# Dividing PSUM in a hybrid mixer trunk: four banks for the dense products, two for the RWKV recurrence, two for the other mixers, in place of three, three and two

## The chip, the cores and the metric

The kernel runs on one core of one Trainium2 chip. The metric is the device time of one execution in microseconds (us). A core has five engines that each work through their own list of instructions: TensorE (PE; its weight loads are PEld), VectorE (DVE), ScalarE (ACT), GpSimd (POOL) and SyncE (SP), which here issues most of the transfers. TensorE writes its results to PSUM, which the kernel uses as eight banks of 128 partitions by 512 floats.

## What is computed

One layer of a trunk with four sequence mixers side by side, for one sequence of 512 tokens and width 1024, all in float32. Cut to what matters:

```python
u = rms_norm(x, g)
fa, fb, fc, fd, gates = split(u @ w_in)         # one wide projection
ya = rwkv7_mix(fa, ...)     # per head: s = s*w + sa (kk*a)^T + v k^T, y = s r
yb = gla_mix(fb, ...)       # gated linear attention in chunks
yc = mlstm_mix(fc, ...)     # matrix LSTM
yd = ssd_mix(fd, ...)       # state space mixer in chunks of 128
h  = x + sum(sigmoid(gate_i) * (y_i @ w_branch_i)) @ w_out
out = rms_norm(h + ffn(rms_norm(h)))            # ffn: 1024 -> 2 x 2816, conv of 3, silu, back
```

## The kernel before, in words

The activations lie with features on the partitions and all 512 tokens along the free axis, so a dense product is one bank: 128 output features by 512 tokens. Each float32 operand is split into a high and a low part in the fast matmul format (hi on ACT at L222, lo on VectorE or POOL at L223), and each product is three matmuls: high by high, high by low and low by high (mm3, L231 to L234). A product `fm` (L305) with 1024 input features is 24 such matmuls of 128x512 into one psd bank; `tm` (L314) makes a product with tokens on the partitions, in 128x256 pieces, with two psd banks at a time (L327 to L329); `branch` (L391) multiplies a mixer's output back to the width (psd<-ohg and olg for GLA, ohr and olr for RWKV, ohm and olm for mLSTM). All dense products take their bank from `pd()`, which is the pool psd.

The mixers stand between the dense products:

- RWKV (`rwkv_half`, L484 to L736) is done in two halves of four heads. Its matmuls take banks from `pr_()`, the pool psr: pair products (L565, L556 to L573, three banks for one pair), the inverse of a triangular matrix by 31 steps on VectorE (L597, L599), its combination (L626, L631), and then the recurrence over eight chunks (L647 to L707). In a step, psx collects the value part (zv, L650) and the carried state (L661), L663 copies it, L687 multiplies it, L690 copies the result to uu, and psy (L673, L678) collects the output, which ACT copies to Yt at L707. The next step's psx is taken right behind the copy at L690, while psy is still open. Behind the last step comes the group norm (L712 to L720), the transposes L725, the gate product L733 and L734, L735.
- GLA (`gla`) takes banks from `pm()`, the pool psm: its chunk products L821 (32x64 pieces) and L835 (64x32 pieces), then L847, L851.
- SSD (`ssd`) and mLSTM (`mlstm`) also use `pm()`, but while `wide` is set, most of their calls go to psr instead (L199 to L203). SSD makes four chunks of 128 tokens; each brings in a decay tile by transfer (sab, L1011, two buffers), works on it (L1033 on POOL and VectorE, exponent on ACT L1034, mask L1035 on POOL, L1044 on VectorE) and multiplies it (L1048), with L1023 as transposes, L1040 and L1041 as the products of the state's keys, L1054 and L1060 as the state's. `ssd_z` (the gate z of SSD, written after the SSD code) is a `tm` product that is emptied at L1077. mLSTM scans its gates (L927 to L932), sends them through DRAM (md, L935, L939), transposes them (L943, L944), makes the weights (L954 to L959), multiplies (L958, L967) and transposes its output (L978).

Everything is written in one function, `tile_trunk_kernel`, in the order RWKV half 0, GLA, SSD, branch 1, z, RWKV half 1, branch 3, mLSTM, branches 0 and 2, output projection, FFN. The order in which an engine gets its instructions is set by a scheduler of the framework, from the priorities that the code gives (`tc.high_priority` with the numbers in Q, L36), from the dependencies, and from which buffers of the pools are free. At about 868 us the three PSUM pools are closed, and the FFN takes all eight banks as one pool (psf).

Of the kernel before, what the change touches and what calls it, by code (L numbers as in the profile page):

```python
# [13 lines left out]
PSUM = bass.MemoryType.PSUM  # L14
# [146 lines left out]
def kernel(ctx: ExitStack, tc: tile.TileContext, A, out):  # L161
# [21 lines left out]
    rpad.tile([P, 56], F32, name="rpad")  # L183
    wp = ctx.enter_context(tc.tile_pool(name="wp", bufs=1))
    ps_ctx = ExitStack()
    psd = ps_ctx.enter_context(tc.tile_pool(name="psd", bufs=3, space=PSUM))
    psr = ps_ctx.enter_context(tc.tile_pool(name="psr", bufs=3, space=PSUM))
    psm = ps_ctx.enter_context(tc.tile_pool(name="psm", bufs=2, space=PSUM))
    dense = [psd]
    dr = ctx.enter_context(tc.tile_pool(name="dr", bufs=1, space=DRAM))  # L190
# [1136 lines left out]
```

## Time and profile before

| what | value |
| --- | --- |
| median of 3 runs | 1225.39 us |
| lowest, highest | 1217.79, 1230.0 us |
| profiled execution | 1220.7 us |
| its span, first to last instruction | 1218.9 us |
| mean granted TensorE clock | 0.981 |
| PE busy | 1166.5 us (96%) |
| DVE busy | 653.7 us (54%) |
| ACT busy | 445.5 us (37%) |
| POOL busy | 333.1 us (27%) |

Busy times count compute instructions alone. A matmul's own duration overlaps its neighbours' on PE, so the time from one to the next is read from a count in a window, not from the mean of one. A window of the trace gives the busy time of each engine between two times; the granted clock is a share of full speed, where 1 is the higher of the two levels (2.4 GHz) and half of it is the lower (1.2 GHz).

### The profile page before, as it was taken

How to read it: one execution, taken by the hardware profiler on the slowest of the kernel's cores; microseconds unless marked ns; L12 is line 12 of the kernel's file. 1: busy time of each engine (PE TensorE's matmuls, PEld its weight loads, DVE VectorE, ACT ScalarE, POOL GpSimd, SP SyncE). 2: the span in 40 equal slices, each digit the busy share in tenths (PEclk: the TensorE clock that was granted, in tenths of full speed). 3: DMA queues.
4: the chain of work that ended last, by engine and by line, in shares of the span. 5: the costliest groups of instructions: out<-in, count | busy, mean ns of one | idle time of the engine just before them, and what ended most of it. 6: DMA issues, size and time to landing. Idle time of an engine off the chain costs nothing.

```text
span 1218.9 us, 17897 instructions
## 1 busy us (share of the span) xinstructions
PE 1166.5 (96%) x6881; PEld 935.6 (77%) x6881; DVE 653.7 (54%) x1090; ACT 445.5 (37%) x820; POOL 333.1 (27%) x287
## 2 busy tenths in 40 slices
PE   5999989999999998989999999999999999999997
PEld 4886865777779965767877877778888888888886
DVE  5257792444675437397224654464556656562323
ACT  4355232223322533223123434342444444442323
POOL 3113110023473246241112363440122222220100
PEclk9998987999999999999999999999999999999999
DMA  5122330122332221323123532463222322323232
GB/s 203 62 88 65 83 85 25 36 83 83 97 104 70 95 90 65 81 78 109 60 72 105 190 112 87 164 217 87 79 95 95 103 96 96 95 95 100 92 102 104
DMA packets 79886, 117.30 MB, mean 96 GB/s; under 512 B 22660, under 2 KB 27172, under 8 KB 79800
## 3 DMA queue, kind: packets, MB, share of 16 engines
q1 hardware_dynamic: 79224, 115.11, 29.7%
q8 instruction: 54, 0.88, 0.3%
q10 hardware_dynamic: 576, 1.05, 0.2%
q14 instruction: 32, 0.26, 0.1%
HBM read 107.93 MB, written 8.19 MB: 95 GB/s over the span
## 4 chain that ended last, share of the span: by engine, by line
PE 74%; DVE 10%; DMA 7%; issue 4%; POOL 2%; ACT 2%; SPq 0%; POOLq 0%; DVEq 0%; ACTq 0%
PE psd L232 16%; PE psd L233 16%; PE psd L234 15%; PE psd L1276 3%; PE psd L1274 3%; PE psd L1275 3%; DVE Mt L597 2%; DVE Mi L599 2%; PE psd L328 2%; PE psd L327 2%; PE psd L329 2%; DVE lo L223 2%; DMA sab<-ad 2%; PE psr L673 1%; DMA raw<-in_wo_dram 1%
## 5 line engine op out<-in xcount | busy, mean ns | idle before, releaser
L223 DVE TENSOR_TENSOR lo<-raw,hi 128x512 fp32r<-128x512 f32 x280 | 226.7, 811 | 299.9 <-ACT hi L222 285.0
L222 ACT CAST hi<-raw 128x512 fp32r<-128x512 f32 x322 | 199.4, 620 | 495.6 <-PE psd L233 300.7
L232 PE MATMUL psd<-uh,hi 128*128 128x512 f32 (+1 forms) x912 | 364.0, 400 | 15.0 <-ACT hi L222 5.1
L234 PE MATMUL psd<-uh,lo 128*128 128x512 f32 (+1 forms) x912 | 362.7, 398 | 5.4 <-DVE lo L223 4.2
L233 PE MATMUL psd<-ul,hi 128*128 128x512 f32 (+1 forms) x912 | 360.5, 396 | 0.2 <-DVE ul L249 0.2
L232 PEld LDWEIGHTS psd<-uh,hi 128*128 128x128 f32 x912 | 173.3, 190 | 57.0 <-ACT hi L222 7.3
L234 PEld LDWEIGHTS psd<-uh,lo 128*128 128x128 f32 x912 | 173.4, 190 | 48.8 <-DVE lo L223 6.2
L233 PEld LDWEIGHTS psd<-ul,hi 128*128 128x128 f32 x912 | 173.4, 190 | 37.3 <-issue 3.1
L223 POOL TENSOR_TENSOR lo<-raw,hi 128x512 fp32r<-128x512 f32 x42 | 57.1, 1360 | 245.8 <-ACT hi L222 176.0
L1263 POOL TENSOR_TENSOR y<-y 128x512 f32<-128x512 f32 x22 | 28.3, 1288 | 172.3 <-DVE y L1257 158.4
L1257 DVE SCALAR_TENSOR_TENSOR y<-psd,pf,y 128x510 f32<-128x510 f32 x88 | 65.8, 749 | 3.0 <-issue 0.3
L1276 PE MATMUL psd<-hi,al 128*128 128x512 f32 x164 | 63.8, 389 | 0.0
L1275 PE MATMUL psd<-lo,ah 128*128 128x512 f32 x164 | 63.8, 389 | 0.0
L1274 PE MATMUL psd<-hi,ah 128*128 128x512 f32 x164 | 57.3, 389 | 0.0
L328 PE MATMUL psd<-lo,uh 128*128 128x256 f32 x192 | 56.1, 292 | 1.0 <-DVE lo L223 1.0
L327 PE MATMUL psd<-hi,uh 128*128 128x256 f32 x192 | 55.5, 289 | 0.0
L329 PE MATMUL psd<-hi,ul 128*128 128x256 f32 x192 | 55.4, 289 | 0.0
L328 PEld LDWEIGHTS psd<-lo,uh 128*128 128x128 f32 x192 | 37.0, 193 | 5.0 <-issue 3.2
L327 PEld LDWEIGHTS psd<-hi,uh 128*128 128x128 f32 x192 | 36.9, 192 | 1.9 <-issue 1.3
L329 PEld LDWEIGHTS psd<-hi,ul 128*128 128x128 f32 x192 | 37.0, 193 | 1.3 <-issue 1.0
L1275 PEld LDWEIGHTS psd<-lo,ah 128*128 128x128 f32 x164 | 30.8, 188 | 6.4
L1276 PEld LDWEIGHTS psd<-hi,al 128*128 128x128 f32 x164 | 30.8, 188 | 6.4
(418 smaller groups left out, 1725.6 us busy)
## 6 DMA issues: line engine op xcount, KB each, us to landing
raw<-in_wfm_dram SPq DMA_DIRECT2D x140, 256.0 KB, 2.6
raw<-in_up_dram SPq DMA_DIRECT2D x88, 256.0 KB, 2.5
raw<-in_dn_dram SPq DMA_DIRECT2D x44, 256.0 KB, 2.5
raw<-in_bp_dram SPq DMA_DIRECT2D x32, 256.0 KB, 2.6
raw<-in_wtm_dram SPq DMA_DIRECT2D x24, 256.0 KB, 2.6
raw<-in_wo_dram SPq DMA_DIRECT2D x16, 256.0 KB, 2.7
gd<-th SPq DMA_DIRECT2D x15, 256.0 KB, 2.1
th<-gd SPq DMA_DIRECT2D x15, 256.0 KB, 3.0
```

Source lines behind the costliest of these rows:

```text
L222: S.copy(hi, raw)
L223: eng.tensor_tensor(lo, raw, hi.bitcast(F32), op=ALU.subtract)
L232: PE.matmul(ps, lh, rh, start=first, stop=False)
L233: PE.matmul(ps, lh, rl, start=False, stop=False)
L234: PE.matmul(ps, ll, rh, start=False, stop=last)
L327: PE.matmul(o, uh[:, k, bs], hi[:, cs], start=first, stop=False)
L328: PE.matmul(o, uh[:, k, bs], lo[:, cs], start=False, stop=False)
L329: PE.matmul(o, ul[:, k, bs], hi[:, cs], start=False, stop=last)
L1257: V.scalar_tensor_tensor(y[:, d:T], ps[:, 0:T - d], col("fcw", k * 44 + n), y[:, d:T], op0=ALU.mult, op1=ALU.add)
L1274: PE.matmul(ps, ah[:, k, bs], hi, start=(k == 0), stop=False)
L1275: PE.matmul(ps, ah[:, k, bs], lo, start=False, stop=False)
L1276: PE.matmul(ps, al[:, k, bs], hi, start=False, stop=(k == NF - 1))
```

## The change

One bank goes from the pool psr to the pool psd; psm keeps its two. The sum stays at eight.

```diff
@@ -183,8 +183,8 @@
     ps_ctx = ExitStack()
-    psd = ps_ctx.enter_context(tc.tile_pool(name="psd", bufs=3, space=PSUM))
-    psr = ps_ctx.enter_context(tc.tile_pool(name="psr", bufs=3, space=PSUM))
+    psd = ps_ctx.enter_context(tc.tile_pool(name="psd", bufs=4, space=PSUM))
+    psr = ps_ctx.enter_context(tc.tile_pool(name="psr", bufs=2, space=PSUM))
     psm = ps_ctx.enter_context(tc.tile_pool(name="psm", bufs=2, space=PSUM))
```

No instruction is added or removed on PE, DVE, ACT or POOL; the scheduler puts them in another order on every engine. Three places of PE's list follow, before and after the change; psd<-uh marks a dense product, psm and psr the mixers' small ones.

GLA's chunk products L835 on PE, in the kernel before:

```order
L835 MATMUL psm<-w 32x32
L233 MATMUL psd<-ul,hi 128x512
L835 MATMUL psm<-w 32x32
L234 MATMUL psd<-uh,lo 128x512
L835 MATMUL psm<-w 32x32
L232 MATMUL psd<-uh,hi 128x512
L835 MATMUL psm<-w 32x32
L233 MATMUL psd<-ul,hi 128x512
L835 MATMUL psm<-w 32x32
```

And the same 32 products of GLA on PE in the changed kernel, with dense rows around them:

```order
L234 MATMUL psd<-uh,lo 128x512
L232 MATMUL psd<-uh,hi 128x512
L233 MATMUL psd<-ul,hi 128x512
L234 MATMUL psd<-uh,lo 128x512
L835 MATMUL psm<-w 32x32 x32
L232 MATMUL psd<-uh,hi 128x512
L233 MATMUL psd<-ul,hi 128x512
```

In the kernel before the single L835 stand one by one between dense matmuls; in the changed kernel this group of 32 is one row.

SSD on PE in the kernel before, from the second chunk's L1048 on:

```order
L234 MATMUL psd<-ohg,lo 128x512
L1048 MATMUL psm<-w,sab 128x64 x8
L1054 MATMUL psm<-w 128x256 x2
L1060 MATMUL psr<-w,sbt 128x256 x2
L1023 MATMUL psr<-cst,w 128x128 x4
L1040 MATMUL psr<-w 128x128 x2
L232 MATMUL psd<-uh,hi 128x512
L233 MATMUL psd<-ul,hi 128x512
L234 MATMUL psd<-uh,lo 128x512
L232 MATMUL psd<-uh,hi 128x512
L233 MATMUL psd<-ul,hi 128x512
L234 MATMUL psd<-uh,lo 128x512
```

SSD on PE in the changed kernel, from the last matmuls of the z product (L327 to L329) on:

```order
L327 MATMUL psd<-hi,uh 128x256
L328 MATMUL psd<-lo,uh 128x256
L329 MATMUL psd<-hi,ul 128x256
L1048 MATMUL psm<-w,sab 128x64 x4
L1060 MATMUL psm<-w,sbt 128x256 x2
L1048 MATMUL psm<-w,sab 128x64 x4
L1040 MATMUL psr<-w 128x128 x2
L1041 MATMUL psr<-cst,w 128x128 x2
L1048 MATMUL psm<-w,sab 128x64 x4
L1054 MATMUL psm<-w 128x256 x2
L1048 MATMUL psm<-w,sab 128x64 x4
L1060 MATMUL psr<-w,sbt 128x256 x2
```

The dense rows (psd<-uh, psd<-ohg) that stood between SSD's matmuls are gone from between them; the z products stand ahead. The next dense row is behind the last L1054:

```order
L1048 MATMUL psm<-w,sab 128x64 x4
L1060 MATMUL psr<-w,sbt 128x256 x2
L1041 MATMUL psm<-cst,w 128x128 x2
L1023 MATMUL psr<-cst,w 128x128 x4
L1048 MATMUL psr<-w,sab 128x64 x8
L1054 MATMUL psr<-w 128x256 x2
L232 MATMUL psd<-uh,hi 128x512
L233 MATMUL psd<-ul,hi 128x512
L234 MATMUL psd<-uh,lo 128x512
```

The L232 at its end is the start of the next RWKV half's projection.

The end of the second RWKV half on PE in the kernel before, from the last dense rows ahead of L725 on:

```order
L232 MATMUL psd<-uh,hi 128x512
L233 MATMUL psd<-ul,hi 128x512
L234 MATMUL psd<-uh,lo 128x512
L725 MATMUL psr<-cst,Yt 128x128 x8
L733 MATMUL psr<-sg,gup 128x512
L232 MATMUL psd<-uh,hi 128x512
L233 MATMUL psd<-ul,hi 128x512
L234 MATMUL psd<-uh,lo 128x512
L232 MATMUL psd<-uh,hi 128x512
L233 MATMUL psd<-ul,hi 128x512
```

The same place in the changed kernel, from the last step of the recurrence on:

```order
L687 MATMUL psr<-xs,MT 64x64 x4
L673 MATMUL psr<-uu,zm_4238 64x64 x4
L678 MATMUL psr<-st,kr 64x64 x4
L725 MATMUL psr<-cst,Yt 128x128 x8
L733 MATMUL psr<-sg,gup 128x512
L232 MATMUL psd<-ohr,hi 128x512
L233 MATMUL psd<-olr,hi 128x512
L234 MATMUL psd<-ohr,lo 128x512
L232 MATMUL psd<-ohr,hi 128x512
L233 MATMUL psd<-olr,hi 128x512
L234 MATMUL psd<-ohr,lo 128x512
L733 MATMUL psr<-sg,gup 128x512
```

In the kernel before dense rows of other products (psd<-uh) stand on both sides of L725; in the changed kernel L725 follows directly behind the recurrence's last L678, and the rows behind it are the RWKV branch's own (psd<-ohr).

## Rows read from the trace of the kernel before

**Rows 1.** The page: busy time of each engine, granted clock in slices.

```profile
PE 1166.5 (96%) x6881; PEld 935.6 (77%) x6881; DVE 653.7 (54%) x1090; ACT 445.5 (37%) x820; POOL 333.1 (27%) x287
...
PEclk9998987999999999999999999999999999999999
```

**Rows 2.** Waits of PE: us in total, times, longest.

```profile
PE psd L232 <- DVE w L899: 5.0, 1, 5.0
...
PE psd L232 <- DVE w L421: 1.9, 1, 1.9
...
PE psr L673 <- DVE uu L690: 1.6, 4, 0.4
```

**Rows 3.** Windows: length, busy of PE, PEld, DVE, ACT, POOL, PEclk, DMA share.

```profile
90.00:120.00 30.00, 28.12 (x218) 20.86 (x218) 23.35 (x36) 15.15 (x26) 11.99 (x11) 0.89 0.24 63
150.00:180.00 30.00, 24.92 (x212) 20.23 (x210) 28.82 (x65) 11.61 (x23) 6.13 (x5) 0.89 0.28 72
188.00:230.00 42.00, 42.00 (x274) 23.39 (x270) 13.59 (x31) 9.32 (x17) 2.54 (x2) 0.76 0.09 26
318.00:379.00 61.00, 56.88 (x299) 47.31 (x298) 46.82 (x84) 18.22 (x39) 42.08 (x34) 0.97 0.33 92
540.00:570.00 30.00, 25.59 (x163) 20.10 (x162) 25.10 (x45) 8.45 (x16) 7.88 (x6) 0.94 0.37 105
650.00:698.00 48.00, 46.63 (x231) 37.26 (x228) 29.81 (x45) 20.15 (x38) 17.30 (x14) 1.00 0.46 152
900.00:930.00 30.00, 30.00 (x134) 24.86 (x133) 17.85 (x23) 14.37 (x23) 6.69 (x6) 1.00 0.29 97
```

**Rows 4.** Groups of PE, 188 to 230 us: count, busy, mean ns, idle.

```profile
L821 PE MATMUL psm<-w 32*64 32x128 f32 x32 | 8.7, 378 | 0.0
L835 PE MATMUL psm<-w 64*32 64x32 f32 x64 | 6.2, 204 | 0.0
L673 PE MATMUL psr<-vp,zm 64*64 64x64 f32 x40 | 2.1, 255 | 0.0
```

**Rows 5.** Groups of PE, 140 to 182 us.

```profile
L821 PE MATMUL psm<-w 32*64 32x128 f32 x80 | 2.9, 275 | 0.0
...
L835 PE MATMUL psm<-w 64*32 64x32 f32 x64 | 0.9, 195 | 0.1
```

**Rows 6.** Chain of waits within 316 to 382 us: start, us, what.

```profile
322.93 7.26 DMA sab<-ad
...
346.98 5.75 DMA sab<-ad
...
365.66 2.72 PE psm L1048 x16
```

**Rows 7.** Timeline of PE around SSD: start, us, what.

```profile
317.64 1.03 PE L725 MATMUL psr<-cst,Yt 128*128 128x128 f32 x8
...
343.75 1.89 PE L1048 MATMUL psm<-w,sab 128*128 128x64 f32 x16
```

**Rows 8.** Groups of PE, 318 to 379 us.

```profile
L234 PE MATMUL psd<-uh,lo 128*128 128x512 f32 x36 | 14.8, 410 | 0.0
```

**Rows 9.** Timeline of PE, end of the second RWKV half and first L967.

```profile
650.82 0.40 PE L678 MATMUL psr<-st,kr 64*64 64x64 f32 x8
...
663.46 1.03 PE L725 MATMUL psr<-cst,Yt 128*128 128x128 f32 x8
...
696.91 0.38 PE L967 MATMUL psr<-mv,w 128*128 128x129 f32 x2
```

**Rows 10.** Groups of DVE and ACT, 560 to 652 us.

```profile
L690 DVE COPY uu<-psr 128x128 f32<-128x128 f32 x8 | 2.3, 291 | 9.4 <-PE psr L687 9.4
...
L707 ACT COPY Yt<-psr 128x128 f32<-128x128 f32 x8 | 2.1, 266 | 8.9 <-DVE st L702 7.3 <-DVE st L705 1.0 <-PE psr L678 0.5
```

**Rows 11.** Timeline of PE and POOL behind the last mLSTM transpose.

```profile
766.80 0.27 PE L978 MATMUL psm<-cst,w 128*128 128x128 f32 x1
...
768.60 1.29 POOL L374 TENSOR_TENSOR olm<-mo,ohm 128x512 fp32r<-128x512 f32 x1 [5.63 <-ACT ohm L373]
```

## The prediction

> **What bounds the kernel now.** I read the page's busy shares first: TensorE is busy 96% of the span, and the granted clock stays near full except in some slices of the first half [rows 1]. Whatever moves the time must therefore add idle time to TensorE, take some away, or change how fast it gets through its own list. The table of waits comes next, because a bank that comes free too late would stand there as a wait of a matmul for the engine that empties a bank. Such rows exist and are small: L232 waits 5.0 us once for the convolution at L899 and 1.9 us for that at L421, both of which read psd banks, and the recurrence waits 1.6 us in all for the copy at L690 [rows 2]. So neither the three dense banks nor the three RWKV banks hold much back as a direct wait. What the waits do not show is the cost of the order itself, and for that I read stretches [rows 3]. 900 to 930 us is a stretch of dense products alone: 134 matmuls in 30 us, 0.224 us each; this is my price of a dense matmul. 188 to 230 us is fully busy and yet slow, with a granted clock of 0.76. 318 to 379 us (SSD) and 650 to 698 us (the end of the second RWKV half and the start of mLSTM) are long chains on other engines which TensorE lives through with 4.1 and 1.4 us of idle, because dense products fill them.
>
> Since the scheduler lays out every engine again when the pools change, the order is the substance of the change. A fourth dense bank lets dense products run ahead; with two psr banks the RWKV steps find a bank later and slide back. In the three pieces of the order dense work has gone out of the two long chains, and small matmuls are put together in batches. I price these in turn, against the profiled execution's 1220.7 us (span 1218.9 plus 1.8 around it).
>
> **Part 1: batches in place of alternation, a gain.** Between 188 and 230 us TensorE has 50 dense matmuls, 32 of L821, 64 of L835 and 128 small ones of the recurrence. The L821 take 8.7 us of busy time, and the L835 6.2 us [rows 4]. Where they stand in batches, 80 of L821 take 2.9 us and 64 of L835 0.9 us [rows 5]. Prices at the batch rate: 50 x 0.224 = 11.2; L821 32 x 0.036 = 1.2; L835 0.9; the recurrence at 0.053 for each of 128 (2.1 us for 40 of L673 [rows 4]), 6.8. That is 20.1, where 42 are used: 21.9 us too many, for the changes of array shape and for the half clock (0.76 where full is 1, so 0.24 x 42 = 10 us of it). Counting all neighbours in the order, changes between a dense matmul and L821 fall from 37 to 7, and those between dense and L835 from 49 to 14: 65 of 86 go. At 65/86 the gain is 16.6; with all of it back, 21.9; if the clock stays low for another reason, only 65/86 of the other 11.9, or 9. I take -18, near the middle of the two cases in which the clock comes back.
>
> **Part 2: SSD without cover, a loss.** SSD is a chain of four chunks whose decay tile (sab) has two buffers. It opens in the space that the first RWKV half leaves, and from that half's L725 (317.64) to the first L1048 (343.75) it needs 26 us: a transfer of 7.26 us, then L1033 and L1035 on POOL and L1044 [rows 6, 7]. The third chunk's transfer is issued as the first L1048 batch ends, at 346.98, and its own L1048 starts at 365.66, so 19 to 20 us pass from one use of a buffer to the next; the fourth chunk's hangs on the second L1048 batch in the same way. In the kernel before, these 61 us are filled by 154 dense matmuls (three lines of 35 or 36, of which one is shown, and three of 16) [rows 8], 154 x 0.224 = 34.5 us. In the changed order the z products stand ahead of the first L1048 and hold all four dense banks, and their evictions (L1077) stand on VectorE behind SSD's own steps; from the first L1048 to the last L1054 no dense matmul is left. I count 15 us of matmuls between L725 and the first L1048 and 15 us of SSD's own after that, 30 together. The chain takes 26 + 20 + 3 = 49 when the fourth chunk follows directly behind the third, and 61 as before. Idle 19 to 31, less the 4.1 there are now: +15 to +27. The chain could even be as short as 40 if half of its 20 us of steps outside the transfers shrink with less foreign work on VectorE and POOL, which gives +6. I take +18, near the 49, as the fourth transfer now finds its buffer as early as the third.
>
> **Part 3: the end of the second RWKV half, a loss.** From the last recurrence matmul (650.82) to L725 (663.46) the group norm takes 12.6 us, and from there the mLSTM scans, the md and row transfers and L954 to L959 follow until L967 (696.91) [rows 9], 46.1 us in all. Part of that is not the chain: between the first L943 and the first L944, which belong together, 46 dense matmuls stand in the order, 10.3 us, which leaves 35.8, and behind L944 come more of them. Alone I put it at 30 us, between 22 (if the scans were ready earlier) and 36. In the changed order only 24 dense matmuls (5.4 us) and 4.5 us of small ones stand there, and the last 18 dense ones also wait for the split of the RWKV result itself. Idle 30 - 9.9 = 20 us, less 1.4: +18.6. The last three steps of the recurrence have lost their fill as well (12 dense matmuls in them), and each must now wait out two copies of 0.29 and 0.27 us [rows 10], at most 3 us in all. The dense products that used to stand here appear before and behind this place, which I count as no gain. Bounds 22 - 9.9 - 1.4 = +11 to +25; I take +16, under the middle since an idle TensorE leaves the other engines free earlier.
>
> **Part 4: smaller terms.** The last mLSTM product now follows directly behind L978; the rows of before give 766.80 for the last L978 and 768.60 + 1.29 for POOL's split behind it [rows 11], 3 us that dense work hides today: +3 (0 to +5). The idle stretches of parts 2 and 3 are each followed by dense work at a clock that had fallen: in 318 to 379 us the mean is 0.97 already with 4.1 us of idle, a loss of 1.8 us. I take +3 for both (0 to +8). The Trainium skill, "TensorE: Matmul & The Clock Gate", section "HAM oscillation — how this bites in real kernels", describes a kernel in which every wait between its groups sent the next group off at the slow clock, so that the price was paid again each time. By that rule the loss of 1.8 us would come at each of the four waits in SSD and once at the RWKV end, 9 us, and the sum would be 6 us higher; the trace agrees so far that 0.97 stands beside 4.1 us of idle. On the other side, in 90 to 120 and 540 to 570 us 1.9 and 4.4 us of idle stand beside a clock of 0.89 and 0.94 (3.3 and 1.8 us); with dense work running ahead I let half of it go, -5 (0 to -9; the whole is 11). VectorE is busy 28.8 of 30 us in 150 to 180 us, so the 5.0 us wait for L899 stays: there VectorE, not a bank, is late. 0.
>
> **Sum.** -18 (part 1) + 18 + 16 + 3 + 3 - 5 = +17, so 1237.7 us for an execution like the profiled one. That execution lies 4.7 us under the median of 1225.39, whose three runs spread over 12 us. I add half of that offset, as I can't tell on which side the next runs fall: 1240. Taking each term at its better bound (-22, +6, +11, 0, 0, -9) gives 1207, all at the worse (-9, +27, +25, +5, +8, 0) 1277; they won't all fall together, and half of each distance, 1225 to 1260, is the forecast's own range.
>
> **Rivals.** First, nothing moves (1225): the chains shrink when they are alone, which leaves the lower bounds, +6 and +11, and with -18, +3, +3 and -2 for the rest +3, or 1223.7, near 1225 with the offset. For it: both chains hold steps of other work on VectorE and POOL (weight splits of L223 among them). Against: the transfers and POOL's steps in them are theirs alone.
> Second, faster (1204): the fourth bank is what the dense products lacked. Then the bank waits of L899 and L421 go (-7), part 1 gives its full -22, the idle of Part 4 goes (-5), and the two chains cost their lower bounds, +17. 1220.7 - 34 + 17 = 1203.7. It decides when the idle time added in SSD and at the RWKV end stays under 24 us together: 1220.7 - 34 + 24 and 2.3 of offset are 1213. The rule of the Trainium skill in "Perfetto Trace Analysis", section "Matmuls", speaks for it: groups should rotate through different banks, so that emptying one overlaps the next group. The trace gives that rule the 7 us above; by it alone the time would be 1214.
> Third, clearly slower (1259): the two psr banks bind the recurrence. Its next product (zv of c+1) takes the bank that the Yt copy and uu copy must first release, 0.27 + 0.29 us and a hop each, near 1.2 us in each of 16 steps, 19 us where no dense work lies beside them. It decides if dense work covers fewer than half of the steps; on top of the forecast its 19 us give 1259. For it: 1.6 us of wait for uu even with three banks. Against: those waits have dense work at hand.
> That the change does nothing is ruled out by the pieces of the order.
>
> **How the numbers follow.** Forecast 0.56, nothing moves 0.19, faster 0.12, clearly slower 0.13. A measurement of this kernel tells about 1% from no change, which is 1213.1 to 1237.6. Of the forecast's own range some two thirds lie above 1237.6, 0.36 of its 0.56, and 0.20 within. With the rivals: slower 0.36 + 0.13 = 0.49, same 0.20 + 0.19 = 0.39, faster 0.12. The range for 8 in 10 takes in the no-change rival and the clearly slower one, and leaves out the faster one and the ends of the bounds: 1210 to 1262.
>
> **What would show it.** Right: TensorE idle of some 18 us between the z products and rwkv_proj(1) with SSD's L1048 spread thin in it; 15 to 20 us idle between the last L678 and L967 of the second half; the stretch of L821 and L835 with a granted clock near 1; L899's wait still there. Wrong: idle of under 10 us in either chain (then they shrink when alone), a half clock that stays through the recurrence in the first half, or waits of L650 and L673 for uu and Yt of more than 10 us in all (then the two RWKV banks bind).

## The result and the profile after

The changed kernel takes 1233.41 us (median of 19 runs, 1228.16 to 1238.18), the kernel before 1222.25 us (19 runs, 1214.53 to 1230.0). The ratio is 1.0092 with a 95% interval of 1.0072 to 1.0112: slower by 0.9%. That is clear of noise, but inside the band of about 1% that the prediction counts as no change. It said 1240 in a range of 1210 to 1262 and put 0.49 on slower (above 1237.6) and 0.39 on same, so of its outcomes the second most likely came, on the side that it had forecast.

The profiled execution (1228.16 us, span 1226.4) is the fastest of the 19, 5.3 us under their median; that of the kernel before lies 1.6 us under its own. So the traces show 7.5 us of the 11.2 us between the medians. The page's shares answer to [rows 1]:

```profile
PE 1156.5 (94%) x6881; PEld 931.7 (76%) x6881; DVE 651.8 (53%) x1090; ACT 445.7 (36%) x820; POOL 332.2 (27%) x287
...
PEclk9999999999997999998998699999999999999999
```

TensorE is busy 10.0 us less, and the span is 7.5 us longer: its idle time has grown from 52.4 to 69.9 us. The work has become cheaper and the waiting longer, which are the two sides of the forecast. The clock's dips have moved too: the slices below 9 stood at 91 to 122 us (projections) and 152 to 213 us (GLA) and stand now at 368 to 399 us (SSD), 552 to 583 us and 644 to 705 us (the RWKV end).

The waits of PE (us in total, times, longest) name both new waits; those for L899 and L421 in [rows 2] are gone:

```profile
PE psm L1048 <- DVE sab L1044: 10.9, 3, 6.2
PE psr L725 <- DVE Yt L720: 10.1, 1, 10.1
PE psr L943 <- DVE ob L735: 2.8, 1, 2.8
...
PE psr L673 <- ACT Yt L707: 1.4, 2, 0.7
...
PE psr L650 <- DVE uu L690: 0.8, 2, 0.4
```

The two lines for the recurrence's copies, Yt and uu, are small, so the two banks of the RWKV pool are hardly waited for as banks.

Windows over the stretches of [rows 3] (length, busy of PE, PEld, DVE, ACT, POOL, granted clock):

```profile
134.00:190.00 56.00, 54.20 (x477) 42.52 (x476) 46.14 (x98) 23.29 (x44) 12.60 (x9) 0.94 0.22 65
338.00:392.00 54.00, 38.90 (x246) 34.62 (x245) 35.41 (x74) 14.60 (x36) 41.39 (x36) 0.86 0.27 69
664.00:699.00 35.00, 20.33 (x107) 14.47 (x103) 20.10 (x29) 10.48 (x20) 15.43 (x13) 0.61 0.10 31
```

The first holds GLA's L821 and 113 of its 128 L835, the second runs from L725 to SSD's last L1054, the third from the last step of the second recurrence to L967. SSD now leaves TensorE idle for 15.1 of 54 us (4.1 of 61 before), the RWKV end 14.7 of 35 us (1.4 of 48), and both have a low clock.

Since all matmuls are the same in both kernels and only their order differs, the two traces can be laid against each other by the amount of matmul work done: each matmul counted at the issue time of its columns (0.227 us for 512, 0.115 for 128 and so on), which sums to 1128.6 us in either. The time at which the changed kernel has a given amount behind it, less that of the kernel before, runs like this (negative: the changed kernel is ahead):

| work done, us | stretch in the changed kernel | difference there | gained or lost since the row above |
| --- | --- | --- | --- |
| 160 | projections, RWKV pair products, first GLA half | -6.6 | -6.6 |
| 260 | second GLA half, first recurrence | -28.8 | -22.2 |
| 360 | rest of the recurrence, z, SSD | -14.3 | +14.5 |
| 580 | second projection and recurrence | -19.1 | -4.8 |
| 660 | its end, group norm, mLSTM's scans | -0.9 | +18.2 |
| 760 | mLSTM's end, branch 2, output projection | +7.5 | +8.4 |
| 1128.6 | FFN | +7.5 | 0 |

The rows rest on these issue times. With others that suit the trace as well, those at 160, 260 and 580 move by 2 us, some by 4, and those at 360, 660 and 760 hardly move. One row hides two parts: at 320 us of work the changed kernel is some 44 us ahead, because dense work that the kernel before does beside SSD is done earlier. The +14.5 is thus a gain of some 15 us ahead of SSD and a loss of some 30 us in it.

### The profile page after: what moved, and what is told of

The parts are those of the page before. It is cut to its first block, busy times and chain, and to the rows that moved or that the text cites. A ratio compares the mean times of both kernels' runs of the same rounds, so it can differ in the third digit from the quotient of the medians.

```text
span 1226.4 us, 17884 instructions
## 1 busy us (share of the span) xinstructions
PE 1156.5 (94%) x6881; PEld 931.7 (76%) x6881; DVE 651.8 (53%) x1090; ACT 445.7 (36%) x820; POOL 332.2 (27%) x287
## 4 chain that ended last, share of the span: by engine, by line
PE 79%; DVE 9%; DMA 4%; POOL 3%; issue 2%; ACT 1%; SPq 0%; POOLq 0%; DVEq 0%; ACTq 0%
PE psd L232 18%; PE psd L233 18%; PE psd L234 18%; PE psd L1275 3%; PE psd L1276 3%; PE psd L1274 3%; DVE Mi L599 1%; PE psd L1223 1%; PE psd L1224 1%; PE psd L1225 1%; PE psr L565 1%; DMA sab<-ad 1%; PE psr L673 1%; DVE Mt L597 1%; DVE lo L223 1%
## 5 line engine op out<-in xcount | busy, mean ns | idle before, releaser
L234 PE MATMUL psd<-uh,lo 128*128 128x512 f32 (+1 forms) x912 | 356.4, 393 | 4.1 <-DVE lo L223 2.3
L232 PE MATMUL psd<-uh,hi 128*128 128x512 f32 (+1 forms) x912 | 358.7, 395 | 0.9 <-ACT hi L222 0.6
L232 PEld LDWEIGHTS psd<-uh,hi 128*128 128x128 f32 x912 | 172.4, 189 | 43.6 <-issue 7.1
L223 POOL TENSOR_TENSOR lo<-raw,hi 128x512 fp32r<-128x512 f32 x42 | 60.5, 1442 | 165.4 <-ACT hi L222 135.3
L329 PE MATMUL psd<-hi,ul 128*128 128x256 f32 x192 | 55.2, 288 | 0.0
L327 PE MATMUL psd<-hi,uh 128*128 128x256 f32 x192 | 54.7, 287 | 0.0
L245 POOL TENSOR_TENSOR gv<-gv,mhalf 128x16 f32<-128x16 f32 x2 | 5.8, 2917 | 137.9 <-DVE gv L244 137.9
L327 PEld LDWEIGHTS psd<-hi,uh 128*128 128x128 f32 x192 | 37.2, 194 | 2.8 <-issue 2.4
L329 PEld LDWEIGHTS psd<-hi,ul 128*128 128x128 f32 x192 | 37.4, 195 | 1.2 <-issue 1.1
L1274 PEld LDWEIGHTS psd<-hi,ah 128*128 128x128 f32 x164 | 30.8, 188 | 6.4
```

The costliest lines, as they stand in the source:

```text
L223: eng.tensor_tensor(lo, raw, hi.bitcast(F32), op=ALU.subtract)
L232: PE.matmul(ps, lh, rh, start=first, stop=False)
L234: PE.matmul(ps, ll, rh, start=False, stop=last)
L327: PE.matmul(o, uh[:, k, bs], hi[:, cs], start=first, stop=False)
L329: PE.matmul(o, ul[:, k, bs], hi[:, cs], start=False, stop=last)
L1274: PE.matmul(ps, ah[:, k, bs], hi, start=(k == 0), stop=False)
```

## Experiments

Time and ratio are against the kernel before, run beside each; the changed kernel itself is at 1233.4 us. A chain of steps on other engines is called covered when dense matmuls stand between its own matmuls on TensorE's list, so that TensorE works while the chain runs. Two kinds of edit are used. An order edge makes a matmul come later than another on TensorE's list without a wait on a semaphore; nothing that is computed changes. It was put in like this (the lines below it in these kernels stand up to 15 further on):

```diff
+    def held(m):
+        for b in marks.get(hold[0], ()):
+            tc.add_manual_dep(m.ins, b.ins.name, mybir.DependencyInfo(mybir.DependencyClass.NoSync, mybir.DependencyReason.DATA), reason="order")
     def mm3(ps, lh, ll, rh, rl, first, last):
-        PE.matmul(ps, lh, rh, start=first, stop=False)
+        m = PE.matmul(ps, lh, rh, start=first, stop=False)
+        if first:
+            held(m)
...
             behind(late, nxt)
+            marks[("rec", hf, c)] = late
```

The other is a high priority on GLA's two loops:

```diff
-                psu = [pm(), pm()]
+                psu = [pm(), pm()]; hg = tc.high_priority(600); hg.__enter__()
...
+                hg.__exit__(None, None, None)
...
-            psa = [pm(), pm()]
+            psa = [pm(), pm()]; hg = tc.high_priority(600); hg.__enter__()
...
-            ats = []
+            hg.__exit__(None, None, None); ats = []
```

### SSD covered again

```diff
         for j in js:
+            hold[0] = {(1, 5): ('rec', 0, 7), (1, 6): ('rec', 0, 7), (1, 7): ('rec', 0, 7)}.get((i, j))
...
-                            PE.matmul(o, uh[:, k, bs], hi[:, cs], start=first, stop=False)
+                            m = PE.matmul(o, uh[:, k, bs], hi[:, cs], start=first, stop=False)
+                            if k == 0 and name == "sz":
+                                hold[0] = ("ssd", (0, 1, 2, 2)[2 * n + b // 2])
+                                held(m)
...
-                PE.matmul(psy[:, h * HD:(h + 1) * HD], ahb[:, h], h3(xd)[:, h], start=True, stop=True)
+                marks[("ssd", b)] = [PE.matmul(psy[:, h * HD:(h + 1) * HD], ahb[:, h], h3(xd)[:, h], start=True, stop=True)]
```

> The changed kernel with an order edge alone: the last three products of branch 1 must not start before the last recurrence step of the first RWKV half, and the four z products not before SSD's L1048 of chunks 0, 1, 2 and 2. That gives SSD 30 us of dense work (11 in the changed kernel) and takes 21 us from the recurrence of the first half. My theory: SSD's idle time falls from 15 to about 4 us and the low clock behind it goes, so 1233 - 11 - 4 = 1218 us. Rival (the dense work only changes places, the first recurrence needs it as much): 1233 us, the idle time turning up between 245 and 323 us.

Measured: 1219.45 us, ratio 0.9979 (0.995 to 1.0008). 14 us come back. By work done, the kernel stands at -25.0 us at 360 in place of -14.3, and the two keep about this distance to the end (-3.7 and +7.5), so the gain lies ahead of 360. The window from 318 to 375 us shows it:

```profile
318.00:375.00 57.00, 52.34 (x337) 45.75 (x335) 43.03 (x82) 17.32 (x38) 40.31 (x34) 0.97 0.34 92
```

4.7 us idle and a clock of 0.97, as in the kernel before. Of the rival there is a part: at 320 us of work this kernel is some 33 us ahead of the kernel before, the changed kernel some 44, so the first recurrence did profit from the dense work that was taken from it, but by less than SSD gains.

### The RWKV end covered again

```diff
         for j in js:
+            hold[0] = ({5: ('rec', 1, 7), 6: ('rec', 1, 7), 7: ('rec', 1, 7)}.get(j) if i == 0 else None)
             nc.sync.dma_start(gd[j], gate(i, j))
```

> The changed kernel with an order edge alone: three of the gate products computed ahead (branch 0, rows 5 to 7) must not start before the last recurrence step of the second RWKV half. The RWKV end then has 24 us of dense work in place of 5, and the recurrence 51 in place of 70. My theory: the 16 us of idle at 660 to 690 us go to about 2 and the low clock behind them too, 1233 - 14 - 4 = 1215 us. Rival (the idle time moves into the recurrence steps, each waiting for its copies): 1230 us or more.

Measured: 1220.66 us, ratio 0.999 (0.9968 to 1.0013): 13 us come back, 5 fewer than forecast. The window over the recurrence's last steps and the RWKV end shows 6.9 us of idle and a clock near full:

```profile
640.00:690.00 50.00, 43.10 (x397) 34.00 (x394) 28.02 (x49) 16.38 (x33) 16.32 (x14) 0.97 0.28 91
```

The recurrence's last steps pay part of what is gained: four waits for Yt of 0.7 to 0.8 us appear between 641 and 652 us.

### Both

The two diffs above in one kernel.

> The order edges of both: SSD and the RWKV end are covered again, with four dense banks and two RWKV banks. My theory: the two losses add up, and what is left is the gain of the batches: 1233 - 15 - 18 = 1200 us, 22 us under the kernel before. Rival (the recurrence with two banks is itself slower): the covers give back half at most, 1218 us or more.

Measured: 1208.58 us, ratio 0.989 (0.9852 to 0.9927). The two nearly add up, 14 + 13 = 27 by the single runs and 24.8 together; the two places give back more than the whole loss, and the kernel is well under the 1218 us that the rival set as its lower limit. TensorE is idle for 52.5 us (span 1210.0, busy 1157.5), as in the kernel before (52.4), where the changed kernel has 69.9. What came back in this trace is idle time and not clock: the trace's clock records lose 32.4 us between 60 and 870 us, 34.1 in the changed kernel and 22.2 in the kernel before. In its waits the price of a bare step with two RWKV banks can be read (here L687, L701 and L664 are L673, L687 and L650 of the kernel before):

```profile
PE psr L687 <- ACT Yt L722: 5.0, 6, 1.4
...
PE psr L701 <- DVE xs L677: 1.7, 5, 0.5
...
PE psr L664 <- DVE uu L704: 1.6, 4, 0.4
```

These are 8.3 us over 15 waits. The first and the third are waits for a bank, 6.6 us over ten; the second is for data and needs no lack of banks. That is the third rival's mechanism at its place, of this size only where the dense work has been taken out of the recurrence.

### The batches alone, with the old banks

The priority's diff above, on the kernel before.

> The kernel before (3, 3 and 2 banks) with a high priority on GLA's L821 and L835 loops alone, so that each group stands together: 4 and 3 changes with dense rows in place of 37 and 49; SSD and the RWKV end keep 39 and 40 us of dense work. My theory (the gain in the changed kernel's first half, 19 us between 160 and 220 us of its trace, comes from the batches): 1222 - 16 = 1206 us. Rival (it comes from dense work that runs ahead in a fourth bank, or the clock falls there whatever the order): within 4 us of 1222 us.

Measured: 1202.43 us, ratio 0.9836 (0.9802 to 0.9871), the fastest kernel of this study, faster than both the kernel before and the changed one. The banks are 3, 3 and 2; only the priority of GLA's two loops is new. Its L821 between 140 and 235 us, against 8.7 us for 32 in [rows 4]:

```profile
L821 PE MATMUL psm<-w 32*64 32x128 f32 x128 | 4.7, 274 | 0.0
```

and the stretch of 188 to 230 us of [rows 3], in which 567 matmuls (not the same ones) are now recorded where it was 274:

```profile
188.00:230.00 42.00, 42.00 (x567) 35.56 (x566) 21.54 (x47) 16.72 (x32) 6.18 (x5) 0.94 0.13 40
```

So the gain belongs to the order of small matmuls, and no fourth dense bank is needed for it. By work done this kernel has gained 18.8 us by 220 and keeps 17.3 to the end. The clock records lose 17.0 us between 60 and 870 us, 22.2 in the kernel before, so by these records some 5 us of the gain are the clock's and the larger part is not.

### Only the RWKV bank taken away

```diff
-    psr = ps_ctx.enter_context(tc.tile_pool(name="psr", bufs=3, space=PSUM))
+    psr = ps_ctx.enter_context(tc.tile_pool(name="psr", bufs=2, space=PSUM))
```

> Three dense banks, two RWKV banks, two others; the eighth bank is unused, so only the RWKV half of the change is made. In its order GLA's small matmuls are batched too (8 and 28 changes with dense rows, against 37 and 49 before), SSD has 23 us of dense work around its L1048 and the RWKV end 24 us. My theory (the loss is the dense work that left SSD and the RWKV end because the fourth dense bank lets it run ahead): about 1217 us, a few us under the kernel before, since the batching gain stays and most of the cover is there. Rival (two RWKV banks bind the recurrence): 1233 us or more, as with the whole change, with waits of L650, L673 for uu and Yt of 10 us and over.

Measured: 1237.1 us, ratio 1.0119 (1.0083 to 1.0154). My number was 20 us off, and the rival's time came out; but the rival's mechanism didn't: the waits for uu are 2.0 us in all, none for Yt. The loss is there without a fourth dense bank, which my theory had made its source. The trace shows where the time is. From 207 to 237 us:

```profile
207.00:237.00 30.00, 27.76 (x243) 24.75 (x243) 9.21 (x18) 6.17 (x12) 4.18 (x2) 0.54 0.22 49
```

Almost all of it is at half clock, from two waits of L626 for its transfer on (2.0 and 1.1 us; 7.1 us of such waits in the kernel), through small matmuls of GLA (L851, L866), L631 and the first steps of the recurrence, with only 19 dense matmuls among them. The clock records lose 39.3 us between 60 and 870 us, 22.2 in the kernel before. The rest lies in SSD (some 20 us by work done from 320 to 360) and in mLSTM's end (+14 from 680 to 720).

### The same with batches

The last diff and the priority's, on the kernel before.

> Three dense banks and two RWKV banks (1237 us) with the high priority on GLA's L821 and L835. The 3, 2 and 2 run lost 36 us to the half clock by its trace, 14 more than the kernel before, 15 of them in one stretch from 207 to 237 us that starts with a wait of L626. My theory (its extra 15 us are that stretch and not the recurrence): time and clock loss move together; if the stretch is gone, 1222 us. Rival (two RWKV banks bind): 1235 us or more also where the clock is high.

Measured: 1222.76 us, ratio 1.0019 (0.9993 to 1.0044). The same window as above:

```profile
207.00:237.00 30.00, 30.00 (x366) 25.66 (x362) 8.23 (x21) 7.93 (x16) 5.46 (x3) 0.94 0.17 49
```

Time (-14.3) and clock loss (39.3 to 22.2, -17.1) moved together, with two RWKV banks in both. The wait for the transfer has not gone, it is longer (5.5 us once, up to 206 us), but 54 dense matmuls are recorded in the 31 us from there, and the clock is low only up to 210.7 us. The priority changes the order as well as the clock, so the two runs don't say how much of the time is the clock's alone. Against 1202.4 us with three RWKV banks and the same batches, though, the bank is worth 20 us. By work done they part at 500 to 520 (8 us, with a wait of 3.9 us of L626 for its transfer) and at 680 to 720 (some 15 us, mLSTM's end), and not in the steps of the recurrence.

### Those that told less

The first gives the RWKV pool its third bank back and takes it from psm, in the changed kernel:

```diff
-    psr = ps_ctx.enter_context(tc.tile_pool(name="psr", bufs=2, space=PSUM))
-    psm = ps_ctx.enter_context(tc.tile_pool(name="psm", bufs=2, space=PSUM))
+    psr = ps_ctx.enter_context(tc.tile_pool(name="psr", bufs=3, space=PSUM))
+    psm = ps_ctx.enter_context(tc.tile_pool(name="psm", bufs=1, space=PSUM))
```

> Four dense banks, three RWKV banks, one for the others: the fourth dense bank without the loss of an RWKV bank. In its order SSD has 47 us of dense work (the changed kernel 11), the RWKV end 10 us (5), the second recurrence 89 us (70); L821 and L835 stand in batches. My theory (loss goes by the missing cover): no SSD loss, the loss at the RWKV end as in the changed kernel, the batching gain, so 1233 - 14 = 1219 us. Rival (the fourth dense bank is good and the second RWKV bank bad, by the 3, 2 and 2 run): 1208 us or less. A single bank for GLA's pairs of banks may cost it some us in either case.

Measured: 1237.3 us, ratio 1.0131 (1.0105 to 1.0158). Neither number came out. SSD lost nothing, as its 47 us of dense work would have it (-6.6 at 340, -7.6 at 380), but some 15 us went in the first recurrence (220 to 260) and some 25 from 580 to 800, at the RWKV end and in mLSTM, which draws on the single psm bank. With that bank in it the run doesn't separate the two halves of the change.

The next holds two gate products of branch 2 behind mLSTM's last transposes, in the kernel with both covers:

```diff
-            hold[0] = ({5: ('rec', 1, 7), 6: ('rec', 1, 7), 7: ('rec', 1, 7)}.get(j) if i == 0 else None)
+            hold[0] = ({5: ('rec', 1, 7), 6: ('rec', 1, 7), 7: ('rec', 1, 7)}.get(j) if i == 0 else {5: ('m', 3), 6: ('m', 3)}.get(j))
...
-                PE.transpose(pst[:, ts_], hv[:, ts_], ident)
+                marks[("m", h)] = [PE.transpose(pst[:, ts_], hv[:, ts_], ident)]
```

> The kernel with both covers (1208.6 us) and one more order edge: two of the gate products computed ahead for branch 2 must not start before mLSTM's last transposes, so that 10 us of dense work stand between these and the product that needs mLSTM's output. My theory: the 4 us that the changed kernel's end of mLSTM loses against the kernel before go, with the low clock behind it: 1203 us. Rival (the dense work is missing beside mLSTM instead, or the wait is for the split): 1208 us or more.

Measured: 1212.91 us, ratio 0.9926 (0.9896 to 0.9956), not told apart from 0.989 (0.9852 to 0.9927). The rival's mechanism is in the trace: the transposes themselves now wait 5.7 us for POOL, where the dense work has gone. By work done the trace gains 4.6 us at 760, but its execution (1207.15 us) is one of the two fastest of its kernel, and that of the kernel with both covers (1211.75 us) lies above its median; the medians go the other way. It stays open whether the edge is worth anything.

The last two put the priority's diff on top of the covers, with all of them and with fewer:

```diff
-            hold[0] = {(1, 5): ('rec', 0, 7), (1, 6): ('rec', 0, 7), (1, 7): ('rec', 0, 7)}.get((i, j))
+            hold[0] = {(1, 6): ('rec', 0, 7), (1, 7): ('rec', 0, 7)}.get((i, j))
...
-                                hold[0] = ("ssd", (0, 1, 2, 2)[2 * n + b // 2])
+                                hold[0] = ("ssd", (0, 0, 1, 2)[2 * n + b // 2])
...
-            hold[0] = ({5: ('rec', 1, 7), 6: ('rec', 1, 7), 7: ('rec', 1, 7)}.get(j) if i == 0 else None)
+            hold[0] = ({6: ('rec', 1, 7), 7: ('rec', 1, 7)}.get(j) if i == 0 else None)
```

> The changed banks (4, 2, 2) with both covers and the high priority on GLA's L821 and L835, which leaves 9 changes with dense rows in place of 21. My theory (the changed order has its batching gain already, the covers have removed its losses, what is left between 1208.6 us and the 1202.4 us of the kernel before with batches is the recurrence with two banks and bare steps, and the end of mLSTM): 1205 us, within 4. Rival (the fourth dense bank has a gain of its own that the alternation hid): under 1198 us, faster than three dense banks with the same batches.

> As the run with both covers and batches, but with one product less held back at each place: SSD has 17 us of dense work (27), the RWKV end 19 (24), the two recurrences 67 and 56 (59 and 51). My theory: the cover at SSD is short again by 10 us, the recurrences have fewer bare steps, together 1211 us. Rival (the recurrences were short of cover, SSD was not): 1202 us or less.

Measured: 1219.66 us, ratio 0.9979 (0.9948 to 1.001), and 1233.13 us, ratio 1.0102 (1.0065 to 1.0139). Both missed. With all covers I was 15 us too low and the rival more; with fewer, 22 us, and the rival more. The priority, which gave 18 us in the kernel before, cost 11 us beside the covers. The window of 200 to 230 us of the run with all covers,

```profile
200.00:230.00 30.00, 25.93 (x239) 22.25 (x238) 11.90 (x30) 4.66 (x10) 2.43 (x1) 0.71 0.24 54
```

has a wait of 3.2 us of L626 for its transfer and a low clock behind it (0.89 in the run with the covers alone), 9 us by work done, and SSD waits 5.6 us for L1044 once. That these came with the new layout is shown; why they did is open. Against each other the two say that one product less at each place costs 13.5 us. By work done the loss at SSD (300 to 340) grows from some 12 to some 18 us, and that from 580 to 740 from some 14 to some 20. Both places are short of cover. The first recurrence gains from the work that it gets back, but less: some 4 us at 300.

## Why the prediction was right, point by point

The sum was +17 on the profiled execution, of which +7.5 was measured (span by span), and +15 on the median (1240 against 1225.4), of which +11 (1233.4 against 1222.3). The direction and the places were right. The forecast loss was a third too large on the medians and more than twice too large between the two profiled executions, of which the changed kernel's is its fastest.

Part 1, batches in place of alternation, -18: measured -22.2 between 160 and 260, and -17.3 in the kernel before by itself, median -18.3. Mechanism and size hold. L821 costs what the batch price said (0.036 us forecast, 4.8 us for 128), L835 more than its 0.014:

```profile
L821 PE MATMUL psm<-w 32*64 32x128 f32 x128 | 4.8, 275 | 0.0
...
L835 PE MATMUL psm<-w 64*32 64x32 f32 x113 | 2.8, 203 | 0.0
```

Part 2, SSD, +18: measured +14.5 with the recurrence ahead of it, and 14 us come back when cover returns. The term was all idle time, and of that there are 11.0 us more (15.1 against 4.1); the rest is the clock (Part 4). The chain took the 54 us that lie between my 49 and 61, while TensorE's own matmuls took 38.9 us in place of my 30. From the chain of waits (start, us):

```profile
340.91 8.12 DMA sab<-ad
...
358.84 1.10 PE psm L1048 x8
...
363.49 5.08 DMA sab<-ad
...
379.73 1.97 PE psm L1048 x8
...
389.25 2.33 PE psr L1048 x16
```

From L725 (337.93) to the first L1048 21 us (forecast 26), from there to the third 20.9 (20), and the fourth 9.5 us behind it (3). The third chunk's transfer was issued behind the first chunk's L1048, and the fourth's within 4.6 us of it. The last two L1048 are parted by steps of VectorE and not by a transfer; these steps I had left out.

Part 3, the RWKV end, +16: measured +18.2, of which 12.8 come back with 24 us of cover. The chain of 30 us from the recurrence to L967 is there:

```profile
667.10 0.58 PE L678 MATMUL psr<-st,kr 64*64 64x64 f32 x8
677.74 1.94 PE L725 MATMUL psr<-cst,Yt 128*128 128x128 f32 x8 [10.05 <-DVE Yt L720]
...
688.15 0.27 PE L943 MATMUL psr<-cst,w 4*128 4x4 f32 x1 [2.82 <-DVE ob L735]
```

10.6 us to L725 and 31.3 to L967 (698.41). Idle grew by 13.3 us (14.7 against 1.4), less than the 18.6 that I had worked out, and the half clock added to it: the mean is 0.61 in the window of 664 to 699 us, and L725 takes 1.94 us where it took 1.03.

Part 4: the clock, +3 with 8 as its bound, was far too small. Half of the time that TensorE was busy within the trace's stretches of half clock is an estimate of what they cost: some 7 us in SSD, 2 in the kernel before, and 8 us at the RWKV end, none before, so +14 for both places. The idle terms, +34 together, came out at +24.3. The two errors nearly cancel, and that the sum of these three terms (37 forecast, 38 by this count) came so near was luck. mLSTM's end, +3, was mis-sized too: +8.4. The wait behind L978 is near the forecast (1.49 us for ohm and 0.4 for olm), but the lines behind it, branch 2 and the output projection, lost as well. The first window is of the changed kernel, the second of the kernel before:

```profile
778.00:808.00 30.00, 26.27 (x106) 20.31 (x105) 16.91 (x19) 11.38 (x19) 19.56 (x16) 0.94 0.44 143
...
766.00:796.00 30.00, 28.19 (x125) 22.74 (x124) 16.31 (x19) 12.15 (x21) 14.50 (x11) 1.00 0.50 166
```

The idle is 3.7 us at a clock of 0.94, where it was 1.8 at 1.00. The edge that was to mend this left it open. The term of -5 for waits that go was too small as well: -6.6 by 160, and -4.8 between 360 and 580. These two errors against each other, with the smaller SSD term, the larger first one and the clock counted within the places, make the 9.5 us between +17 and +7.5.

Of the signs that were named ahead, the idle time at both places came (15.1 for some 18, 14.7 for 15 to 20), the stretch of L821 and L835 has a clock of 0.94, and the waits for uu and Yt stayed small. One failed: the wait for L899, which I expected to stay because VectorE is late there, is gone. A bank is not what took it away, for it is gone as well with three dense banks (the run with only the RWKV bank taken away) and there with four (1.1 us in the run with 4, 3 and 1): it goes by the order.

Of the rivals, the first (nothing moves) fell by the interval, and its chains did not shrink to +6 and +11: their idle time grew by 11.0 and 13.3 us. The second (the fourth bank is what the dense products lacked) was to be decided by the idle time added at both places, under 24 us; it is 24.3, at the limit, and yet the time is 20 us over the 1213 that this limit stood for. With the covers put back the time was 1208.6 us, but the batches alone gave more without the bank (1202.4 us). The third fell in the changed kernel (waits for Yt and uu of 2.6 us in all) and showed itself in the run with both covers (6.6 us of waits for a bank). There its price was near: a bare step waits 0.69 us for Yt and 0.39 for uu, 1.1 us, where I had 1.2.

The Trainium skill's rule of rotating groups through different banks ("Perfetto Trace Analysis", "Matmuls") gave nothing for the dense products that a run shows: the kernel with three dense banks and batches is faster than any with four. On the clock, the Trainium skill ("TensorE: Matmul & The Clock Gate", "HAM oscillation — how this bites in real kernels") has a kernel in which every wait between groups was paid for again at the slow clock. The trace agrees: both new gaps were followed by half clock, with means of 0.86 and 0.61 over the windows, and the 9 us that the prediction worked out by it lie nearer to the 14 above than its own 3.

The step from the order to its cause was the weak one, though of the terms only the -5 of Part 4 rested on it. I put the loss on the fourth dense bank that lets dense work run ahead, and the run with two RWKV banks and three dense ones came out at 1237 us without it. What the runs show is less: in the changed kernel the two uncovered chains make the loss, with the half clock behind them, and taking the RWKV bank alone moves the order enough to lose as much, in part at other places. With equal batches the third RWKV bank is worth 20 us. The fourth dense bank alone was not run, since the run with 4, 3 and 1 also takes a psm bank. Each edit lays out the whole list anew, so a difference of some 10 us between two such kernels need not come from the place that was edited; for the two covers the work done says that it does. Which step of the scheduler turns a bank into these orders was not tried.

## What to carry to other kernels

Where a scheduler lays out the list, a change of a pool's size is a change of the whole order: read the new order for chains that have lost their cover and for small matmuls that alternate with large ones, and price these, before any wait for a bank. When such a change gains in one place and loses in another, look for the gain by itself: a priority on two loops gave 1.6% with the old banks, where the new banks lost 0.9%.

## What was not expected

A low clock can last far longer than the wait it follows: in the run with only the RWKV bank taken away, waits of 2.0 and 1.1 us up to 210.5 us stand in a stretch of 30 us with a clock of 0.54, by which some 14 us were lost (an estimate from the clock alone), while TensorE counted as busy for 27.8 of them. With batches a longer wait at the same place, 5.5 us, left a clock of 0.94 over the same 30 us; TensorE then had 54 dense matmuls where it has 19 here. And the spread of a kernel's own executions goes with the clock: over the 19 runs of the changed kernel, time and mean granted clock correlate with -0.90, from 1228.16 us at 0.971 to 1238.18 us at 0.963, and a straight line through all 19 has some 10 us for 0.01.
